# First stage of a hybrid attention step: eight cached sequences compressed one by one in 64 units

## The chip, the cores and the metric

The kernel runs on one core of a Trainium2 chip. The metric is device time of one execution in microseconds (us), as the median of several runs; lower is better. The engines are named as in the profile: PE (TensorE, the matrix products) with PEld (its weight loads), DVE (VectorE), ACT (ScalarE), POOL (GpSimd) and SP (SyncE, which here only issues DMAs). Each engine takes its instructions from a queue of its own, in the order in which the program put them there.

## What is computed

One decode step of a one-layer model: a prompt of 512 rows and eight sample sequences of 8 rows, each sample with 2048 cached tokens in 16 pages of 128 tokens. What matters here is the compression of the cached keys and values of the sparse attention branch, and the start of the layer:

```python
def compress_blocks(x, pos, w1, w2):          # x: 2048 cached tokens of one sequence, 2 groups of 64
    xc = x.reshape(b, n_chunk, 16, NSA_GROUPS, HEAD_DIM)
    lead  = einsum('bncgd,cdh->bngh', xc + pos[0], w1[0])
    trail = einsum('bncgd,cdh->bngh', xc + pos[1], w1[1])
    return einsum('bngh,hd->bngd', silu(lead[:, :-1] + trail[:, 1:]), w2)
...
mod = silu(c) @ w_ada + b_ada                 # conditioning: shift, scale, gate
h = rms_norm(x, norm1_g) * (1.0 + sc1) + sh1  # prompt and sample rows
z = h @ w_in
```

Keys and values (kv = 0, 1) of eight sequences go through `compress_blocks`. Everything after `z` (three attention branches, the output projection, the MLP) is untouched by the change.

## The kernel before, in words

The first stage (`first_stage`, line 512) interleaves two jobs. One is the compression of the eight cached sequences; the other is the work that the projection `z` needs: the norm of x, its transposition, and the first eight blocks of the conditioning `mod` (called ada). The compression is cut into **units**, listed in `self.units` (line 548). A unit is a set of sequences `bs`, a quarter j of the 16 token positions, and kv. The first 16 units handle one sequence each (sequences 0 and 1, eight units per sequence), the other 24 handle two at a time (2 and 3, 4 and 5, 6 and 7): 40 units.

What one unit does:

- `cmp_order` (line 447, DVE): a copy `ro<-cpg` of 128x1024 elements for each sequence, which brings the page tile `cpg` into the order that the transposes want; once for two units (k and v).
- `rows_turn` (line 456): four transposes on PE for each sequence, into a PSUM tile `ct`; then, for each of two halves a, ACT rounds the half to `xh` (128x256) and DVE takes the rest `xl` = ct - xh (128x256). `xh` and `xl` lie in a ring of two units.
- `cmp_hidden` (line 473): twelve products on PE (four weights times the three terms high*high, low*high, high*low), accumulated in the PSUM tile `hid`. A product has 256 columns for one sequence, 512 for two.

The main loop (line 623) runs over u. In round u the program issues `rows_turn(u + 1)`, then `cmp_hidden(u)`, then the jobs in `todo[u]`. PE's order is therefore ct(u+1), hid(u), ct(u+2), hid(u+1) and so on, with the extra products of `todo` between them. `cmp_order(u + 2)` comes before `rows_turn(u + 1)`, except where the next unit begins with a new set of sequences ((u + 2) % 8 == 0, line 636): there it comes after `rows_turn(u + 1)`. With `behind()` (line 535) an instruction is kept behind the last split (`xh`, `xl`) that was issued so far on ACT and on DVE; before the change that holds for `cmp_order` in the units up to 15 and at every change of sequences.

`todo` (lines 570 to 621) holds by unit: the norm of the five tiles of x (`norm`: a square with sum on ACT, 128x1024; some ten small steps and a 128x1024 scaling on DVE), their transposes (`turned`: eight products `nt`, two copies), the ada blocks (`ada_first`, `ada_end`, lines 316 and 303; 1 MB of w_ada each, asked for on POOL's queue), `modulate` (line 752, DVE), and for each two sequences the silu (`cmp_act`: two ACT passes and one DVE pass over 128x512, for k and for v), the second product (`cmp_out`, `co`), the key norm and its transpose (`cmp_keys`, `kct`). `pages(b)` asks on SP's queue for the 16 pages of sequence b, into one of four `cpg` tiles. `asked(f)` (line 581) puts a one-element POOL copy that reads `xl` ahead of an issue on POOL's queue, so that the issue waits for that unit.

The end of the stage is the **seam** (line 2095), called at u == 38, with two units left. It frees the stage's tiles, asks for the first columns of w_in (`winr`), and splits h, eight row blocks `h2[k]`, each one ACT pass (128x576) and two DVE passes (128x512 and 128x64, line 777), and `winh`, `winl` in two halves (one ACT pass and one DVE pass of 128x1056 each). Pins fix the order on ACT and DVE: `h2[0..2]` behind the splits of unit 38, then, behind those of unit 39, half 0 of w_in, `h2[3..4]`, half 1, `h2[5..7]`. The first tile of `z` (24 products, three for each k) follows hid(39) on PE.

Of the kernel before, what the change touches and what calls it, by code (L numbers as in the profile page):

```python
# [18 lines left out]
NB = 8  # L19
# [26 lines left out]
class Step:  # L46
# [465 lines left out]
    def first_stage(self, pl, pe, hf, seam):  # L512


        nc = self.nc
        self.chain = ""
        self.sideb = self.mmb
        self.w1raw, self.cpg, self.ros, self.hid, self.adas = [], {}, {}, {}, {}
        xs = []

        def load_x():
            k = len(xs)
            xs.append(pe.tile([P, D], F32, tag="x", bufs=3, name=f"x{k}"))
            self.dma("gpsimd", xs[k][:TILES[k][1]], self.x_rows(k))

        def norm(k):
            with self.tc.issue_after(self.last_high):
                self.norm_scaled(xs[k], 0, k, xs[k], pl.tile([P, D], BF16, tag="csx", name=f"sq{k}"))

        def turned(k):  # L530
            t0, m = TILES[k]
            for h in range(2):
                self.copy(hf[:, 4 * h:4 * h + 4, t0:t0 + m], self.norm_turned(xs[k], 0, k, h))

        def behind():
            both = ExitStack()
            for i in (self.last_high, self.splits[-1]):
                both.enter_context(self.tc.issue_after(i))
            return both

        def pinned(f):
            def g():
                with behind():
                    f()
            return g


        self.units = [(b // 2, bs, j, kv) for b, bs in ((0, (0,)), (1, (1,)), (2, (2, 3)), (4, (4, 5)), (6, (6, 7)))
                      for j in range(4) for kv in range(2)]
        self.page_rows()  # L550
        for b in range(4):
            self.cmp_tile(pe, b)
        self.cmp_raw(pe, 0)

        warm = self.small.tile([P, 1], F32, tag="warm", bufs=1, name="warm")
        nc.vector.memset(warm, 0.0)
        self.act(warm, warm, AF.Tanh)
        self.cmp_pages("sync", 0, slice(0, 8))
        self.cmp_pages("scalar", 0, slice(8, 16))
        self.cmp_raw(pe, 1)  # L560
        self.cmp_pages("sync", 1)
        self.cmp_weights(pl)
        self.ada_start()
        self.constants()
        self.late_constants()
        self.cmp_pages("sync", 2)
        self.cmp_pages("sync", 3)

        ada, ends = [4, 0, 5, 1, 6, 2, 7, 3], {}
        todo = {u: [] for u in range(40)}  # L570
        todo[9] += [pinned(self.ada_silu)]
        todo[18] += [pinned(self.cmp_second_half)]
        todo[10] += [self.constants_turned, self.ada_turned, lambda: ends.update(b=self.cmp_bias(pe))]
        todo[12] += [lambda: self.cmp_bias_end(ends["b"])]

        for k, u in enumerate((19, 21, 23, 25, 27)):
            todo[u - 2] += [lambda k=k: norm(k)]
            todo[u] += [lambda k=k: turned(k)]
        pages = lambda b: lambda: (self.cmp_tile(pe, b), self.cmp_pages("sync", b))
        wada = lambda k: lambda: self.ada_first_load(pe, ada[k])  # L580
        def asked(f):
            def g():

                x = self.ring[0][1]
                c = nc.gpsimd.tensor_copy(warm, x[:, 0, 0:1].bitcast(F32))
                with self.tc.issue_after(c.ins):
                    f()
            return g

        todo[8] += [pages(4)]  # L590
        todo[9] += [asked(self.cmp_second)]
        todo[14] += [pages(5)]
        todo[15] += [asked(load_x)]
        todo[16] += [load_x, load_x]
        todo[17] += [asked(wada(0))]
        todo[19] += [load_x]
        todo[21] += [load_x]
        todo[23] += [asked(wada(1))]
        todo[24] += [self.late_loads]
        todo[20] += [pages(6)]  # L600
        todo[22] += [pages(7)]
        for k, u in enumerate((22, 25, 27, 29, 31, 32, 34, 35)):
            todo[u] += [lambda k=k: ends.update({k: self.ada_first(pe, ada[k])})]
            todo[u + 1] += [lambda k=k: ends[k]()]
            if k > 1:
                todo[(23, 26, 28, 30, 32, 33)[k - 2]] += [wada(k)]
            if k % 2:
                todo[max(u + 2, 28)] += [lambda k=k: self.modulate(0, hf, range(k - 1, k + 1))]
        self.lfg = {}
        for y, u in enumerate((25, 28)):  # L610
            todo[u] += [pinned(lambda y=y: self.stage_logf(pe, y))]
            todo[u + 2] += [lambda y=y: self.store_logf(y)]
        for i in range(3):
            for kv in range(2):
                todo[8 * i + 14 + kv] += [lambda i=i, kv=kv: self.cmp_act(pl, i, kv)]
        for i in range(3):
            for kv in range(2):
                todo[8 * i + 18 + kv] += [lambda i=i, kv=kv: self.cmp_out(pl, i, kv)]
            todo[8 * i + 21] += [lambda i=i: self.cmp_keys(i)]
        self.cmp_order(pl, 0)  # L620
        self.cmp_taps(0)
        self.rows_turn(0)
        for u in range(40):
            if u % 2 == 0 and u + 2 < 40 and (u + 2) % 8:
                with behind() if u + 2 < 16 else nullcontext():
                    self.cmp_order(pl, u + 2)
            if u + 1 < 8:
                with behind():
                    self.cmp_taps(u + 1)
            if u + 1 < 40:  # L630
                self.rows_turn(u + 1)
            if u == 37:
                self.behind38 = self.splits[-1], self.last_high
            if u == 38:
                seam()
            if (u + 2) % 8 == 0 and u + 2 < 40:

                with behind():
                    self.cmp_order(pl, u + 2)
            self.cmp_hidden(u)  # L640
            for f in todo[u]:
                f()
        self.r1 = self.keep.tile([P, 5 * D], F32, tag="r1", bufs=1, name="r1w")
        with behind():
            for kv in range(2):
                self.cmp_act(pl, 3, kv)
        self.sideb = self.stackb = self.trb
# [1425 lines left out]
    def run(self):  # L2073
# [10 lines left out]
        hf = self.adw[:, 0:NK * NT].rearrange("p (k t) -> p k t", k=NK)  # L2084
# [7 lines left out]
        pl, pe = self.pool("pl", lctx), self.pool("pe", actx)  # L2092
        h2 = []

        def seam():
# [15 lines left out]

            self.wraw = {}
            self.win_load(self.pw, 0)
            rows(self.behind38, range(3))
            for i in range(2):
                self.win_split(self.pw, 0, i, last)
                rows(last, ((3, 4), (5, 6, 7))[i])

        self.first_stage(pl, pe, hf, seam)
        lctx.close()  # L2120
# [133 lines left out]
```

## Time and profile before

| | |
|---|---|
| median of 3 runs | 1231.15 us (1231.12 to 1231.8) |
| the profiled execution, its own time | 1231.5 us |
| its span in the profile | 1229.7 us |
| granted TensorE clock, mean | 0.994 |
| PE busy | 1186.9 us (97%) |
| PEld busy | 1022.7 us (83%) |
| DVE busy | 684.9 us (56%) |
| ACT busy | 513.6 us (42%) |

Rows of the timeline read: start (us from the span's start), length in us, engine, line, operation, output<-input, partitions x elements and count; in brackets how long the engine had been idle before it, and what it had waited for. A row with xN merges N instructions; lengths of PE rows contain the time that a result takes to come out, so starts are compared, not lengths. In rows of the waits stand: who waited for whom, total us, times, longest us.

### The profile page before, as it was taken

Reading aid. Unit: us, or ns where it says so; the run is one execution under the profiler, and the core shown is the slowest. Engines: PE = TensorE matmul, PEld = TensorE weight load, DVE = VectorE, ACT = ScalarE, POOL = GpSimd, SP = SyncE. Lnnn points to the kernel's source line nnn. Section 1 sums busy time; section 2 is a strip of 40 time slices with the busy share of each in tenths; the row PEclk is TensorE's granted clock in tenths of the full one; section 3 lists DMA queues with packets and bytes.
Section 4 is the critical chain, followed back from the end, with each engine's and each line's share of the span. In section 5 each row is a group of like instructions: output and inputs, shape, how many; then the busy total and the mean of one; then the engine's idle time right before and its main releaser. Section 6 shows DMA issues by size and latency. Waiting matters only on the chain.

```text
span 1229.7 us, 24815 instructions
## 1 busy us (share of the span) xinstructions
PE 1186.9 (97%) x9475; PEld 1022.7 (83%) x9475; DVE 684.9 (56%) x1875; ACT 513.6 (42%) x1152; POOL 131.2 (11%) x144
## 2 busy tenths in 40 slices
PE   3899999999999989999999999999999999999998
PEld 3888789999666556666799999998989989899896
DVE  3688785676788845555543445654343433434546
ACT  2455453454777744454432333365423213232230
POOL 1012100001211120000200000001102011020110
PEclk9999999999999899999999999999999999999999
DMA  9589547794866449789763234115314223142202
GB/s 208 160 246 272 161 145 235 245 319 151 287 208 200 132 138 308 255 264 295 172 165 94 78 93 128 29 52 155 103 43 130 69 70 103 53 119 70 69 18 77
DMA packets 170201, 188.11 MB, mean 153 GB/s; under 512 B 16185, under 2 KB 149762, under 8 KB 167906
## 3 DMA queue, kind: packets, MB, share of 16 engines
q1 hardware_dynamic: 157890, 167.13, 44.6%
q0 software_dynamic: 6880, 16.25, 4.4%
q10 hardware_dynamic: 5312, 3.15, 1.2%
q8 instruction: 75, 1.23, 0.4%
q14 instruction: 44, 0.36, 0.1%
HBM read 176.48 MB, written 30.90 MB: 169 GB/s over the span
## 4 chain that ended last, share of the span: by engine, by line
PE 85%; DVE 5%; DMA 4%; SPq 3%; ACT 2%; issue 1%; DVEq 0%; ACTq 0%
PE up L77 17%; PE dn L77 17%; PE mg L77 8%; PE z L77 7%; PE hid L77 5%; PE wo L77 4%; PE br L77 4%; PE ss L77 4%; SPq L155 3%; PE k L83 2%; PE ct L83 2%; PE so L77 2%; DMA cpg<-in_cache_nsa_kv 2%; PE ada L77 1%; PE sp L83 1%
## 5 line engine op out<-in xcount | busy, mean ns | idle before, releaser
L77 PE MATMUL z<-winh,h 128*128 128x264 f32 (+1 forms) x576 | 111.0, 286 | 0.3
L2024 POOL TENSOR_TENSOR u<-u 128x576 f32<-128x576 f32 x32 | 53.4, 1669 | 409.3 <-ACT u L112 318.2
L77 PEld LDWEIGHTS z<-winh,h 128*128 128x128 f32 x576 | 91.7, 190 | 2.1 <-DVE h L777 0.9
L77 PE MATMUL z<-winl,h 128*128 128x264 f32 (+1 forms) x320 | 88.2, 284 | 0.2 <-DVE winl L131 0.2
L100 DVE TENSOR_TENSOR acc<-acc,dn 128x512 f32<-128x512 f32 x60 | 39.8, 685 | 73.0 <-PE dn L77 73.0
L77 PE MATMUL mg<-hH,wmh 128*128 128x288 f32 x256 | 75.9, 298 | 2.0 <-ACT wmh L112 2.0
L77 PE MATMUL mg<-hH,wml 128*128 128x288 f32 x256 | 75.9, 298 | 0.9 <-DVE wml L131 0.9
L112 ACT ACTIVATE xh<-ct 128x256 fp32r<-128x256 f32 x128 | 48.0, 385 | 59.2 <-PE ct L83 35.8
L77 PE MATMUL mg<-hL,wmh 128*128 128x288 f32 x256 | 72.6, 294 | 0.0
L131 DVE TENSOR_TENSOR xl<-ct,xh 128x256 fp32r<-128x256 f32 x128 | 51.6, 420 | 19.4 <-ACT xh L112 17.7
L777 DVE TENSOR_TENSOR u<-u,u 128x512 fp32r<-128x512 f32 x64 | 27.4, 469 | 60.7 <-ACT u L112 60.7
L77 PEld LDWEIGHTS z<-winl,h 128*128 128x128 f32 x320 | 60.6, 190 | 0.4 <-DVE winl L131 0.4
L83 PE MATMUL ct<-identF,ro 128*128 128x128 f32 x256 | 36.3, 281 | 22.7 <-DVE ro L115 22.1
L83 PEld LDWEIGHTS ct<-identF,ro 128*128 128x128 f32 x256 | 29.6, 146 | 26.6 <-DVE ro L115 18.7
L77 PEld LDWEIGHTS mg<-hH,wmh 128*128 128x128 f32 x256 | 48.6, 190 | 2.4 <-ACT wmh L112 2.2
L77 PEld LDWEIGHTS mg<-hH,wml 128*128 128x128 f32 x256 | 48.5, 189 | 1.1 <-DVE wml L131 1.1
L131 DVE TENSOR_TENSOR wml<-wmr,wmh 128x1024 fp32r<-128x1024 f32 x14 | 17.1, 1224 | 56.0 <-ACT wmh L112 55.9
L112 ACT ACTIVATE u<-up 128x256 f32<-128x256 f32 (+1 forms) x96 | 27.8, 325 | 48.7 <-PE up L77 48.7
L77 PEld LDWEIGHTS mg<-hL,wmh 128*128 128x128 f32 x256 | 47.2, 188 | 0.1
L77 PE MATMUL hid<-xh,w1hlk 128*128 128x512 f32 (+1 forms) x160 | 45.0, 369 | 0.1
L77 PE MATMUL hid<-xh,w1hlv 128*128 128x512 f32 (+1 forms) x160 | 43.9, 360 | 0.5 <-ACT xh L112 0.5
L1700 DVE CUSTOM_DVE_ANT_0 sS<-ss,scr 128x512 f32<-128x512 f32 x32 | 22.1, 691 | 30.2 <-PE ss L77 30.2
(951 smaller groups left out, 3584.1 us busy)
## 6 DMA issues: line engine op xcount, KB each, us to landing
adw<-in_w_ada SPq DMA_DIRECT2D x16, 1024.0 KB
foxD<-in_cache_fox_kv SPq DMA_DIRECT2D x128, 128.0 KB
wur<-in_w_up SPq DMA_DIRECT2D x32, 512.0 KB
wdr<-in_w_down SPq DMA_DIRECT2D x32, 512.0 KB
cpg<-in_cache_nsa_kv SPq DMA_DIRECT2D x120, 128.0 KB
fr<-foxD SPq DMA_DIRECT2D x28, 512.0 KB
sr<-in_cache_nsa_kv SPq DMA_DIRECT2D x112, 128.0 KB
wada<-in_w_ada POOLq DMA_DIRECT2D x8, 1024.0 KB, 6.3
```

Of the source, the lines that this page charges most:

```text
L77: ins = self.nc.tensor.matmul(out, a, b, start=start, stop=stop, skip_group_check=True)
L83: ins = self.nc.tensor.transpose(out, in_, self.identF[:n, :n])
L100: self.nc.vector.tensor_tensor(out, a, b, op=op)
L112: return self.nc.scalar.activation(out, in_, f, **kw)
L131: self.splits.append((eng or self.nc.vector).tensor_tensor(l, x, h.bitcast(F32), op=OP.subtract).ins)
L155: self.issued[eng] = getattr(self.nc, eng).dma_start(out, in_).ins
L777: self.packed = (eng or self.nc.vector).tensor_tensor(h2[:, o:o + n], x[:, i:i + n], h2[:, i:i + n].bitcast(F32), op=OP.subtract).ins
L1700: self.nc.vector.tensor_tensor_reduce(self.S[u], pb, self.ramp[:, 512 * i:512 * i + 512], 1.0, LOW, OP.add, OP.max, self.stat[b][0][:, i / ...
L2024: nc.gpsimd.tensor_tensor(u[j], u[j], u[j], op=OP.mult)
```

## The change

All eight sequences get units of their own: 64 units, sequence b in units 8b to 8b + 7, so all products `hid` have 256 columns. The jobs in `todo` are placed anew over 64 units: norms at 19, 23, 27, 31, 35 and their transposes three units later, ada blocks at 29 to 56, silu and second product every 16 units. Pages of sequences 5 to 7 are asked for at units 14, 22, 30. Counted in units, the rows of x and the blocks of w_ada are asked for further ahead of their use. `cmp_order` of all units is now kept behind the last splits. The seam is called at u == 62, again with two units left; `h2[0]` is pinned behind the splits of unit 61, `h2[1]` behind those of unit 62, and half 0 of w_in, `h2[2..4]`, half 1 and `h2[5..7]` behind those of unit 63.

```diff
-        self.units = [(b // 2, bs, j, kv) for b, bs in ((0, (0,)), (1, (1,)), (2, (2, 3)), (4, (4, 5)), (6, (6, 7)))
-                      for j in range(4) for kv in range(2)]
+        self.units = [(b // 2, (b,), j, kv) for b in range(NB) for j in range(4) for kv in range(2)]
+        N = len(self.units)
...
-        for k, u in enumerate((19, 21, 23, 25, 27)):
-            todo[u - 2] += [lambda k=k: norm(k)]
+        for k, u in enumerate((22, 26, 30, 34, 38)):
+            todo[u - 3] += [lambda k=k: norm(k)]
             todo[u] += [lambda k=k: turned(k)]
...
-        todo[8] += [pages(4)]
+        for b in range(4, NB):
+            todo[8 * (b - 4) + (8 if b == 4 else 6)] += [pages(b)]
         todo[9] += [asked(self.cmp_second)]
-        todo[14] += [pages(5)]
         todo[15] += [asked(load_x)]
-        todo[16] += [load_x, load_x]
-        todo[17] += [asked(wada(0))]
-        todo[19] += [load_x]
-        todo[21] += [load_x]
-        todo[23] += [asked(wada(1))]
-        todo[24] += [self.late_loads]
-        todo[20] += [pages(6)]
-        todo[22] += [pages(7)]
-        for k, u in enumerate((22, 25, 27, 29, 31, 32, 34, 35)):
+        todo[16] += [load_x]
+        todo[18] += [load_x]
+        todo[20] += [asked(wada(0))]
+        todo[23] += [load_x]
+        todo[25] += [asked(wada(1))]
+        todo[27] += [load_x]
+        todo[28] += [self.late_loads]
+        for k, u in enumerate((29, 34, 39, 43, 47, 50, 53, 56)):
             todo[u] += [lambda k=k: ends.update({k: self.ada_first(pe, ada[k])})]
             todo[u + 1] += [lambda k=k: ends[k]()]
-            if k > 1:
-                todo[(23, 26, 28, 30, 32, 33)[k - 2]] += [wada(k)]
+            if k < 6:
+                todo[u + 1] += [wada(k + 2)]
             if k % 2:
-                todo[max(u + 2, 28)] += [lambda k=k: self.modulate(0, hf, range(k - 1, k + 1))]
+                todo[max(u + 2, 40)] += [lambda k=k: self.modulate(0, hf, range(k - 1, k + 1))]
...
-        for u in range(40):
-            if u % 2 == 0 and u + 2 < 40 and (u + 2) % 8:
-                with behind() if u + 2 < 16 else nullcontext():
+        for u in range(N):
+            if u % 2 == 0 and u + 2 < N and (u + 2) % 8:
+                with behind():
                     self.cmp_order(pl, u + 2)
...
-            if u == 37:
-                self.behind38 = self.splits[-1], self.last_high
-            if u == 38:
+            if N - 4 <= u < N - 2:
+                self.ahead.append((self.splits[-1], self.last_high))
+            if u == N - 2:
                 seam()
...
-            rows(self.behind38, range(3))
+            rows(self.ahead[0], (0,))
+            rows(self.ahead[1], (1,))
             for i in range(2):
                 self.win_split(self.pw, 0, i, last)
-                rows(last, ((3, 4), (5, 6, 7))[i])
+                rows(last, ((2, 3, 4), (5, 6, 7))[i])
```

## The prediction on record

> **What bounds the kernel now.** I read the page's busy shares first, then busy time by stretches, then the waits and PE's timeline for the first 190 us. The sequence of PE's products behind the first stage is the same in both programs, so the change is decided before the first product of `z`.
>
> ```profile
> span 1229.7 us, 24815 instructions
> ...
> PE 1186.9 (97%) x9475; PEld 1022.7 (83%) x9475; DVE 684.9 (56%) x1875; ACT 513.6 (42%) x1152; POOL 131.2 (11%) x144
> ...
> 62.50:100.00 37.50, 37.44 (x230) 31.19 (x229) 31.59 (x118) 22.25 (x53) 6.97 (x12) 1.00 0.89 247
> ...
> PE ct L83 <- DVE ro L115: 22.1, 4, 18.7
> ```
>
> PE is busy for 97% of the span, and in a stretch inside the stage for 37.44 of 37.5 us. Of PE's waits in the first 190 us only one group is large, transposes that wait for DVE's copy `ro`: 22.1 us, of which 18.7 are the start, before any page has been copied. That leaves 3.4 us. No row of x and no block of w_ada stands among what PE waited for, so asking for them sooner has nothing to remove. The stage is a chain of PE products with few holes; what counts is PE's work, and whether ACT and DVE have each unit ready in time.
>
> **The change part by part.**
>
> *Pace of PE.* In the next rows x4 is a unit of one sequence, x8 one of two.
>
> ```profile
> 39.94 0.60 PE L83 MATMUL ct<-identF,ro 128*128 128x128 f32 x4
> ...
> 40.30 0.48 PE L77 MATMUL hid<-xh,w1hlk 128*128 128x256 f32 x2
> ...
> 41.83 0.60 PE L83 MATMUL ct<-identF,ro 128*128 128x128 f32 x4
> ...
> 65.56 1.06 PE L83 MATMUL ct<-identF,ro 128*128 128x128 f32 x8
> ...
> 66.38 0.71 PE L77 MATMUL hid<-xh,w1hlv 128*128 128x512 f32 x2
> ...
> 69.24 1.04 PE L83 MATMUL ct<-identF,ro 128*128 128x128 f32 x8
> ...
> 160.52 1.04 PE L83 MATMUL ct<-identF,ro 128*128 128x128 f32 x8
> ...
> 164.21 0.38 PE L83 MATMUL kct<-identF,knn 128*128 128x128 f32 x2
> ```
>
> Narrow unit: 41.83 - 39.94 = 1.89 us, of it 0.36 for the transposes and 1.53 for the twelve 256-column products. Wide unit: 3.68 us from 65.56 to 69.24, 2.86 of it for the twelve 512-column products. Of the 21 such starts of wide units with nothing else between them (first and last above, 3.68 and 3.69) the mean is 3.73. The other products between the units (`nt`, `co`, `kct`, `ada`, `adat`) are the same in number. From the first hid of unit 16 to the first of `z`, before: 22 x 3.73 + 2 x 2.86 = 87.8 us. After: 48 x 1.53 + 46 x 0.36 = 90.0. The cost is **+2.2 us**.
>
> A rule speaks against narrow products here. The Trainium skill, "TensorE: Matmul & The Clock Gate", section "Back-to-back issue gap", has sustained spacings of about 81 ns at 128 columns and 131 ns at 512. An estimate from these two figures puts 256 columns near 98 ns, so two narrow products would take 1.49 times one wide one and the change would cost 24 x 2.86 x 0.49 = 34 us. The trace disagrees: 2 x 1.53 / 2.86 = 1.07. I go by the trace.
>
> *The start of the first pair.* Before, ct(16) needs copies for both sequences:
>
> ```profile
> 54.61 0.60 PE L83 MATMUL ct<-identF,ro 128*128 128x128 f32 x4
> ...
> 57.80 0.63 PE L83 MATMUL ct<-identF,ro 128*128 128x128 f32 x4 [1.14 <-DVE ro L115]
> ...
> 59.23 0.63 PE L83 MATMUL ct<-identF,ro 128*128 128x128 f32 x4 [0.79 <-DVE ro L115]
> ...
> 61.64 1.06 PE L83 MATMUL ct<-identF,ro 128*128 128x128 f32 x8 [0.35 <-DVE xl L131]
> ...
> 62.46 0.71 PE L77 MATMUL hid<-xh,w1hlk 128*128 128x512 f32 x2
> ...
> 56.60 0.42 DVE L131 TENSOR_TENSOR xl<-ct,xh 128x256 fp32r<-128x256 f32 x1 [0.45 <-ACT xh L112]
> ...
> 56.97 0.69 DVE L115 COPY ro<-cpg 128x1024 f32<-128x1024 f32 x1
> ...
> 58.39 1.29 DVE L115 COPY ro<-cpg 128x1024 f32<-128x1024 f32 x2 [0.73 <-DMA cpg<-in_cache_nsa_kv]
> ```
>
> The first half of ct(16) starts at 57.80, the second waits for the second copy (page data of sequence 3: DVE idle 0.73) until 59.23, and ct(17) waits 0.35 for `xl`; the first product of unit 16 starts at 62.46. After: ct(16) at 57.80 as before, 0.36 + 1.53 (hid 15) + 0.36 (ct 17), hid(16) at 60.05. **-2.4 us**. The 1.14 us at 57.80 stay: that copy is behind the last split of unit 15 in both programs.
>
> *The same wait at five more places.* The three rows of DVE say what that wait is: the copy for a new sequence stands behind the last `xl` of the unit before (56.60, then 56.97), and ct(16) follows the copy's end. From ct(15) to ct(16) are 57.80 - 54.61 = 3.19 us instead of 1.89: **1.30 us** lost. The chain that ends there, for a narrow unit:
>
> ```profile
> 40.58 0.39 ACT L112 ACTIVATE xh<-ct 128x256 fp32r<-128x256 f32 x1 [0.59 <-PE ct L83]
> ...
> 41.45 0.39 ACT L112 ACTIVATE xh<-ct 128x256 fp32r<-128x256 f32 x1 [0.49 <-DVE xl L131]
> ...
> 41.00 0.42 DVE L131 TENSOR_TENSOR xl<-ct,xh 128x256 fp32r<-128x256 f32 x1
> ...
> 41.87 0.42 DVE L131 TENSOR_TENSOR xl<-ct,xh 128x256 fp32r<-128x256 f32 x1 [0.45 <-ACT xh L112]
> ```
>
> Within a unit ACT and DVE take turns, each waiting for the other: `xh` 40.58, `xl` 41.00, `xh` 41.45 (0.49 idle for `xl`), `xl` 41.87 to 42.29. That is 2.35 us after its transposes began at 39.94. Add 0.69 for a copy and the hand-over, and the next sequence's transposes cannot start before 3.1 to 3.2 us, while PE needs them after 1.89. A wide unit gave PE 3.7 us. In DVE's queue of the changed program the first copy for sequences 3, 4, 5, 6 and 7 stands right behind the last `xl` of units 23, 31, 39, 47 and 55. What hides it is only what PE has between: `nt` of one x tile ahead of ct(24), ct(32) and ct(40), and `adat` ahead of ct(32) and ct(56); nothing ahead of ct(48).
>
> ```profile
> 96.27 1.04 PE L83 MATMUL nt<-identF,x 128*128 128x128 f32 x8
> ...
> 97.14 0.38 PE L83 MATMUL adat<-identF,adap 128*128 128x128 f32 x2
> ...
> 97.36 1.04 PE L83 MATMUL ct<-identF,ro 128*128 128x128 f32 x8
> ```
>
> `nt` takes 97.14 - 96.27 = 0.87, `adat` 0.22. Left over: 0.43, 0.21, 0.43, 1.30, 1.08, together **+3.45 us**. Bounds: half of it, 1.7, if PE is itself held up shortly before and the copies catch up; 5 x 1.30 = 6.5 if nothing covers (`nt` needs the scaled x, which stands in the same DVE queue).
>
> *Bursts with a shorter look-ahead.* The last `xl` of a narrow unit is ready at 2.35 us, and the first product that reads it (the sixth of twelve) comes at 2 x 1.89 - 1.53 + 0.6 = 2.85 us after that unit's transposes began: 0.5 us to spare. Into this go, over 48 units, five norms, three key norms, four `modulate` and the silus:
>
> ```profile
> 33.08 0.50 PE L77 MATMUL hid<-xh,w1hlv 128*128 128x256 f32 x2 [0.46 <-ACT xh L112]
> ...
> 94.84 1.05 ACT L112 ACTIVATE sq<-x 128x1024 bf16<-128x1024 f32 x1
> ...
> 102.92 0.74 DVE L104 TENSOR_SCALAR x<-x,nrs 128x1024 f32<-128x1024 f32 x1
> ```
>
> One square holds ACT for 1.05 us, one scaling DVE for 0.74. Neither fits into 0.5 us. Nothing in the old trace shows them in narrow units; the nearest row is in units 1 to 7, which also carried a split of the weights each: there PE lost 0.46 us (at 33.08) in seven units. 48 units at that rate: **+3.2 us**; that is my value. Below it 0: DVE has free time over the stage, and 20 us of extra products lie on PE in the same units. Above, twice as much, 6.4.
>
> *The end of the stage.* Both programs call the seam two units before the end, but a unit is half as long now.
>
> ```profile
> 164.43 1.03 PE L83 MATMUL ct<-identF,ro 128*128 128x128 f32 x8
> ...
> 170.88 0.40 PE L77 MATMUL z<-winh,h 128*128 128x264 f32 x2
> ...
> 174.95 0.41 PE L77 MATMUL z<-winh,h 128*128 128x264 f32 x2
> ...
> 177.86 1.00 PE L77 MATMUL co<-w2rawk,r1w 128*128 128x64 f32 x8
> ...
> 167.47 1.08 ACT L112 ACTIVATE winh<-winr 128x1056 fp32r<-128x1056 f32 x1
> ...
> 168.44 1.25 ACT L112 ACTIVATE h<-adw 128x576 fp32r<-128x576 f32 x2
> ...
> 171.23 1.25 DVE L131 TENSOR_TENSOR winl<-winr,winh 128x1056 fp32r<-128x1056 f32 x1
> ...
> 172.40 2.29 DVE L777 TENSOR_TENSOR h<-adw,h 128x512 fp32r<-128x512 f32 x6
> ```
>
> Before, the last transposes start at 164.43; the last `xh` is done when `winh` starts at 167.47, 3.41 us ahead of `z` at 170.88. From there ACT and DVE have two halves of w_in (1.1 to 1.25 us each) and five row blocks (0.6 each on ACT, 2.29 / 3 = 0.76 on DVE) to split, down to 174.69 on DVE. The first tile of `z` runs behind them: 174.95 - 170.88 = 4.07 us instead of the next tile's 177.86 - 174.95 = 2.91. After, ct(63) starts 0.36 + 2 x 1.53 = 3.42 us ahead of `z`, and its last `xh` ends 1.90 later (39.94 to 41.45 + 0.39), so only 1.52 us are left instead of 3.41: 1.9 us later. Six row blocks instead of five are behind it: 0.76 more. And h2[1] now stands on ACT ahead of that `xh`: 0.6. Sum **+3.3 us**; from 1.9 (start alone) to 4.0 (h2[1] costs its DVE passes too).
>
> *Moved issues.* A 1 MB block of w_ada takes this long on POOL's queue from issue to landing:
>
> ```profile
> wada<-in_w_ada POOLq DMA_DIRECT2D x8, 1024.0 KB, 6.3
> ```
>
> Each block is asked for one unit after the sum that frees its place and is used at least five units later, 9.5 us of PE time against 6.3: hidden, with some 3 us to spare; if the cover goes, PE waits for the difference. The rows of x are half as large. On POOL the later issues (conditioning, gathers) stand in the same order behind them. On SP the pages of sequences 6 and 7 are asked for when the copies of 2 and 3 free their tiles, 26 narrow units (49 us) ahead of use; before, those of 7 came 10 wide units (37 us) ahead, and PE waited for neither. The stores of log forget values stand ahead of `winr` as before. I take all of these at nothing.
>
> *Sum.* -2.4 + 2.2 + 3.45 + 3.2 + 3.3 = **+9.75 us**. The profiled execution took 1231.5 us with a span of 1229.7 us; the median is 0.35 lower, 1231.15. 1231.5 + 9.75 - 0.35 = **1240.9 us**.
>
> **The rivals.**
>
> - *Only the end costs.* The five boundary waits and the bursts vanish behind PE's other products; 1231.15 - 0.2 + 3.3 = 1234.3 us. For it: DVE and ACT are not full. Against: ct(48) and ct(56) have next to nothing ahead of them.
> - *Look-ahead too short throughout.* Each of 14 bursts costs 0.5 us and no boundary is covered: -0.2 + 6.5 + 7 + 3.3 = 16.6, 1247.8 us. Against: units 1 to 7 lost only 0.46.
> - *Bare rate (the faster side).* The tile of `z` above ran 24 products of 264 columns in 2.91 us, 0.121 each. If narrow units ran so, a pair would take 2 x (12 x 0.121 + 0.36) = 3.62 instead of 3.73: 24 x 0.11 = 2.6 us gained, with the 2.4 at the start 5 us: 1226.1 us. It decides if boundaries, bursts and end together stay under 2.5 us. Against: narrow units with nothing in the way took 1.89, and the end alone is put at 3.3.
> - *Only PE's work changes.* -2.4 + 2.2, nothing else: 1231 us. That is also the case in which asking sooner and spreading out does what it says and no wait is added.
> - *Weight loads no longer hidden.*
>
> ```profile
> L77 PEld LDWEIGHTS hid<-xh,w1hlk 128*128 128x128 f32 x160 | 28.0, 197 | 3.7 <-ACT xh L112 0.4
> ```
>
> A load takes 197 ns; twelve of them 2.4 us against 1.53 measured for a narrow unit's products. If PE had to wait for them: 0.8 x 48 = 40 us more, about 1271. Against: the narrow units of the trace hide them. The rule of the Trainium skill quoted above, from "TensorE: Matmul & The Clock Gate", points this way.
>
> **How the numbers follow.** Forecast 0.66, only the end 0.12, look-ahead too short 0.09, bare rate 0.08, PE's work alone 0.04, weight loads 0.01. A measurement of this kernel tells about 0.2% (2.5 us) from no change. Faster by more than that: 0.08. Within it: 0.04. Slower: 0.88. Low end of the range: -0.2 + 1.7 + 0 + 1.9 = 3.4, with the rival at 1234.3 taken in: 1234 us. High end: -0.2 + 6.5 + 6.4 + 4.0 = 16.7: 1248 us. Outside lie the faster side and little else, about 0.15. The likeliest case's own range is 1236 to 1246.
>
> **What the next profile would show.** All 768 `hid` products with 256 columns, 1.5 us for twelve. Transposes that wait for `ro` at eight starts of PE instead of four, most for about 1 us, the longest at ct(48) and ct(56). PE idle on `xh` or `xl` in units 17 to 39 by a few tenths each. The first tile of `z` over 6 us long, with starts that follow DVE's h splits. No wait of PE for a DMA. I am wrong if the first tile of `z` takes under 4.5 us, or if ct(48) starts within 2.2 us of ct(47); and, the other way, if PE waits for x, w_ada or pages.

## The result, and the profile after

The changed kernel takes 1243.08 us (median of 4 runs, 1241.84 to 1244.66), the kernel before, run beside it, 1231.13 us (4 runs, 1228.1 to 1231.8). The ratio is 1.0103, 95% interval 1.0082 to 1.0123: **slower by about 1%**, 12 us; forecast were 9.75 us.

The page of the changed kernel opens with its span and the busy shares:

```profile
span 1241.1 us, 25367 instructions
...
PE 1190.7 (96%) x9763; PEld 1038.5 (84%) x9763; DVE 687.3 (55%) x1875; ACT 515.1 (42%) x1152; POOL 130.8 (11%) x144
```

PE has 288 more instructions and is busy for 3.8 us more; the span grew by 11.4. Two thirds of the loss is therefore PE standing still. Where it stands still, PE's timeline shows (start, length, ..., in brackets the idle time and what ended it):

```profile
54.93 0.60 PE L83 MATMUL ct<-identF,ro 128*128 128x128 f32 x4
58.13 0.63 PE L83 MATMUL ct<-identF,ro 128*128 128x128 f32 x4 [1.15 <-DVE ro L115]
60.01 0.60 PE L83 MATMUL ct<-identF,ro 128*128 128x128 f32 x4
60.36 0.48 PE L77 MATMUL hid<-xh,w1hlk 128*128 128x256 f32 x2
...
66.37 1.10 PE L77 MATMUL co<-w2rawk,cst 128*128 128x64 f32 x8 [0.52 <-DVE w2rawk L104]
...
86.10 1.09 PE L83 MATMUL nt<-identF,x 128*128 128x128 f32 x8 [0.61 <-DVE x L104]
...
105.71 1.09 PE L83 MATMUL nt<-identF,x 128*128 128x128 f32 x8 [0.76 <-DVE x L104]
...
116.53 0.44 PE L83 MATMUL kct<-identF,knn 128*128 128x128 f32 x2 [1.01 <-DVE ntt L100]
...
120.36 0.63 PE L83 MATMUL ct<-identF,ro 128*128 128x128 f32 x4 [0.86 <-DVE ro L115]
...
136.30 0.60 PE L83 MATMUL ct<-identF,ro 128*128 128x128 f32 x4
139.50 0.63 PE L83 MATMUL ct<-identF,ro 128*128 128x128 f32 x4 [1.15 <-DVE ro L115]
...
176.83 0.60 PE L83 MATMUL ct<-identF,ro 128*128 128x128 f32 x4
...
180.88 0.40 PE L77 MATMUL z<-winh,h 128*128 128x264 f32 x2
...
187.73 0.41 PE L77 MATMUL z<-winh,h 128*128 128x264 f32 x2
```

The reader is to see four things. The start of the third sequence is short now: ct(16) at 58.13, the first product of unit 16 at 60.36. At 139.50 stands ct(48), 3.20 us after ct(47) instead of 1.89, waiting for `ro`. Between lie waits of 0.5 to 1 us for `w2rawk`, for the scaled `x` and for the key norm (`ntt`). And the first tile of `z` runs from 180.88 to 187.73, 6.85 us instead of 4.07.

For the third point, the same four products in the kernel before, none of which waits:

```profile
73.01 1.10 PE L77 MATMUL co<-w2rawk,cst 128*128 128x64 f32 x8
...
86.69 1.04 PE L83 MATMUL nt<-identF,x 128*128 128x128 f32 x8
...
105.12 1.04 PE L83 MATMUL nt<-identF,x 128*128 128x128 f32 x8
...
126.90 0.44 PE L83 MATMUL kct<-identF,knn 128*128 128x128 f32 x2
```

For the fourth, DVE after the change. The row blocks of h stand between and behind the two halves of w_in, and the second tile starts at 187.73, 0.27 us after the last of them is done (185.16 + 2.30 = 187.46), as it did before (174.69 and 174.95):

```profile
180.61 1.26 DVE L131 TENSOR_TENSOR winl<-winr,winh 128x1056 fp32r<-128x1056 f32 x1 [0.73 <-ACT winh L112]
181.79 2.29 DVE L776 TENSOR_TENSOR h<-adw,h 128x512 fp32r<-128x512 f32 x6
184.00 1.26 DVE L131 TENSOR_TENSOR winl<-winr,winh 128x1056 fp32r<-128x1056 f32 x1
185.16 2.30 DVE L776 TENSOR_TENSOR h<-adw,h 128x512 fp32r<-128x512 f32 x6
```

ct(16) itself comes 0.32 us later in this execution, before anything differs, so I count from ct(16). In these terms (differences of starts in the timelines; "tile" is the time from the first product of one tile of `z` to the first of the next):

| | ct(16) to z | first tile | second tile | sum |
|---|---|---|---|---|
| before | 113.08 | 4.07 | 3.72 | 120.87 |
| after | 122.75 | 6.85 | 4.42 | 134.03 |

The stage lost 13.2 us, while the whole span lost 11.4: in these two executions the rest of the program took 1.8 us less after the change. Most of that lies 420 us later, where the branch mixing `mg` waits for a split weight, first before, then after the change:

```profile
PE mg L77 <- ACT wmh L112: 2.0, 1, 2.0
```

```profile
PE mg L77 <- ACT wmh L112: 0.7, 1, 0.7
```

Ahead of it the shift of PE's products had grown to 14.0 us (a wait for a window load `wr`: 2.75 instead of 2.19 us), behind it it is 11.4 and stays there to the end. It is tempting to say that a PE that arrives later waits less, but the other traces don't bear this out. What is late is a load of w_in, for which ACT is idle ahead of the split (6.32 us before, 5.08 after). The wait of `mg` behind it is 0.9 us in the experiment "the earlier copy in the kernel before", where `z` starts at 171.18, and 2.3 us in "four sequences narrow", where it starts at 174.50. From the third tile of `z` to the end, the thirteen profiles of this case take between 1047.7 and 1051.1 us, with the same PE products there: 1051.1 before, 1048.9 after, 1048.2 in that kernel with the earlier copy. So the 1.8 us are within what this part differs by from profile to profile; that the change gives them back is not shown. Below I therefore judge the first stage by the trace and the whole by medians.

### The profile page after: what moved, and what is told of

Its sections match the earlier page's. It is cut to its first block, busy times and chain, and to the rows that moved or that the text cites. A ratio compares the mean times of both kernels' runs of the same rounds, so it can differ in the third digit from the quotient of the medians.

```text
span 1241.1 us, 25367 instructions
## 1 busy us (share of the span) xinstructions
PE 1190.7 (96%) x9763; PEld 1038.5 (84%) x9763; DVE 687.3 (55%) x1875; ACT 515.1 (42%) x1152; POOL 130.8 (11%) x144
## 4 chain that ended last, share of the span: by engine, by line
PE 84%; DVE 5%; DMA 5%; ACT 3%; SPq 2%; issue 1%; DVEq 0%; ACTq 0%
PE up L77 16%; PE dn L77 16%; PE mg L77 8%; PE z L77 8%; PE wo L77 4%; PE br L77 4%; PE ss L77 4%; PE hid L77 3%; DMA cpg<-in_cache_nsa_kv 3%; PE k L83 2%; PE so L77 2%; SPq L155 2%; PE ada L77 2%; PE ct L83 1%; PE sp L83 1%
## 5 line engine op out<-in xcount | busy, mean ns | idle before, releaser
L83 PE MATMUL ct<-identF,ro 128*128 128x128 f32 x256 | 40.0, 281 | 24.8 <-DVE ro L115 23.8
L77 PE MATMUL hid<-xh,w1hlk 128*128 128x256 f32 x256 | 51.8, 300 | 0.1
L77 PE MATMUL hid<-xh,w1hlv 128*128 128x256 f32 x256 | 50.3, 292 | 0.5 <-ACT xh L112 0.4
L77 PEld LDWEIGHTS hid<-xh,w1hlk 128*128 128x128 f32 x256 | 40.4, 195 | 0.4 <-ACT xh L112 0.4
```

Of the source, the lines that this page charges most:

```text
L77: ins = self.nc.tensor.matmul(out, a, b, start=start, stop=stop, skip_group_check=True)
L83: ins = self.nc.tensor.transpose(out, in_, self.identF[:n, :n])
```

## The experiments

My theory was the prediction's: narrow products cost PE almost nothing, and the loss is waits, at the boundaries between sequences, behind bursts on ACT and DVE, and at the seam. The rival: narrow units are slower by themselves (PE, ACT and DVE can't supply them), and a wait taken away shows up again elsewhere.

**Copies ahead of the splits.** In the changed kernel the first copy of sequences 3 to 7 is put ahead of the splits of the unit before:

```diff
-            if u % 2 == 0 and u + 2 < N and (u + 2) % 8:
+            if u % 2 == 0 and u + 2 < N and ((u + 2) % 8 or u + 2 > 16):
...
-            if (u + 2) % 8 == 0 and u + 2 < N:
+            if (u + 2) % 8 == 0 and u + 2 <= 16:
```

> The changed kernel with one edit: the first copy ro for sequences 3 to 7 is issued one unit earlier, as for all other units (before the transposes of the unit ahead, not behind their splits). Wait theory (the loss is made of waits at the changes of sequence, of bursts on ACT and DVE, and of the late seam): the five waits at ct(24), ct(32), ct(40), ct(48), ct(56), 4.15 us in the changed kernel's trace, go; the first product of z moves from 180.9 to about 176.8 us, the median from 1243 to about 1239. Pace theory (narrow units are slow in themselves, the waits only show where PE is ahead of its supply): the wait turns up elsewhere in the same units, z starts later than 179.5, median within 1.5 us of 1243.

Measured: 1240.04 us (4 runs, 1238.73 to 1242.55; ratio to the kernel before 1.0085, 1.0053 to 1.0118). ct(16) to z fell from 122.75 to 120.81. PE's timeline:

```profile
116.81 0.44 PE L83 MATMUL kct<-identF,knn 128*128 128x128 f32 x2 [1.66 <-DVE ntt L100]
...
135.62 0.60 PE L83 MATMUL ct<-identF,ro 128*128 128x128 f32 x4
137.51 0.60 PE L83 MATMUL ct<-identF,ro 128*128 128x128 f32 x4
...
157.27 0.41 PE L83 MATMUL kct<-identF,knn 128*128 128x128 f32 x2 [0.61 <-DVE knn L100]
```

ct(47) and ct(48) are 1.89 us apart: the largest boundary wait has gone to nothing, and those ahead of ct(40) and ct(56) with it; only ct(24), which also waits for `nt`, kept its 0.4. Together 3.5 us went. But the key norm's transpose now waits 1.66 instead of 1.01, and another 0.61, and two units lost 0.2 to 0.3: 1.8 us came back. Both theories have a part: the waits are what the prediction said, and removing them moves a copy ahead of other work that was itself only just in time.

**The last pair in wide units.** Sequences 0 to 5 one by one, 6 and 7 together, 56 units, the seam's pins as before the change. The last four ada blocks move with it, one of them to the place ahead of ct(48), and the copies `ro` within the wide units are free of the pin to the last splits again:

```diff
-        self.units = [(b // 2, (b,), j, kv) for b in range(NB) for j in range(4) for kv in range(2)]
+        self.units = [(b // 2, bs, j, kv) for b, bs in [(b, (b,)) for b in range(6)] + [(6, (6, 7))] for j in range(4) for kv in range(2)]
...
-        for k, u in enumerate((29, 34, 39, 43, 47, 50, 53, 56)):
+        for k, u in enumerate((29, 34, 39, 43, 46, 48, 50, 51)):
...
-                with behind():
+                with behind() if u + 2 < 48 else nullcontext():
...
-            rows(self.ahead[0], (0,))
-            rows(self.ahead[1], (1,))
+            rows(self.ahead[1], range(3))
...
-                rows(last, ((2, 3, 4), (5, 6, 7))[i])
+                rows(last, ((3, 4), (5, 6, 7))[i])
```

> The changed kernel with sequences 6 and 7 compressed as a pair again (48 narrow units and 8 wide ones, 56 in all), the seam two wide units before the end and pinned as before the change. Wait theory: the first tile of z takes about 4.1 us instead of 6.85, the hold-ups by h2[0] and h2[1] in the last units (0.47 and 0.63) and the wait at ct(56) (1.1) go, some 0.5 us come back from the pace: median near 1237.5. Pace theory: the eight pairs give back a third of the loss up to z, 3 to 4 us, and the first tile of z stays at 6.5 us or more: median near 1239.5.

Measured: 1235.71 us (9 runs, 1234.09 to 1237.54; ratio 1.0043, 1.0024 to 1.0062). PE at the seam:

```profile
170.35 1.04 PE L83 MATMUL ct<-identF,ro 128*128 128x128 f32 x8
...
176.81 0.40 PE L77 MATMUL z<-winh,h 128*128 128x264 f32 x2
...
180.88 0.40 PE L77 MATMUL z<-winh,h 128*128 128x264 f32 x2
```

From 176.81 to 180.88 the first tile of `z` takes 4.07 us, as before the change: the whole 2.8 us at that place go with a wide last unit and the old pins. The run doesn't tell these two apart, so how much of the 2.8 us is the shorter time behind the last transposes alone stays open. ct(16) to z fell to 119.17, the sum to the third tile to 126.96. One pair out of three made wide gave back 7.1 of the stage's 13.2 us, because the boundaries ahead of ct(48) and ct(56) and the seam are all in it; ahead of ct(48) there is now an ada block as well. The median is 1.8 us lower than the wait theory had it.

**No norm.** This kernel leaves out the norm of x in the first stage:

```diff
         def norm(k):
             with self.tc.issue_after(self.last_high):
-                self.norm_scaled(xs[k], 0, k, xs[k], pl.tile([P, D], BF16, tag="csx", name=f"sq{k}"))
+                pass
```

> The changed kernel without the norm of x in the first stage (x is transposed and used as it was loaded: no square, no small steps, no scaling). It leaves out five bursts on ACT (1.2 us each) and DVE (some 2 us each). Wait theory: PE's waits for the scaled x (0.61 and 0.76) go and the wait at ct(40) falls from 1.0 to 0.4 or less: z starts 2 to 3 us sooner than 180.9. Rival (bursts hide in DVE's free time, the waits come from the change of sequence alone): under 1 us sooner.

Measured: 1242.2 us in one run; ct(16) to z 120.14, 2.6 less, as the wait theory had it. On PE:

```profile
114.06 0.44 PE L83 MATMUL kct<-identF,knn 128*128 128x128 f32 x2
...
117.54 0.63 PE L83 MATMUL ct<-identF,ro 128*128 128x128 f32 x4 [0.53 <-DVE ro L115]
```

The waits of `nt` for `x` are gone, and so is the 1.01 us of `kct`, whose small steps had stood behind the norm's on DVE (0.45 of it appears at a `hid` instead). ct(40) waits 0.53 instead of 0.86. So the norms alone are worth 2.6 us of the stage in narrow units. The span of this one execution is only 0.7 us shorter (1240.4), as the part behind the stage took longer.

**Loads asked for later.** In the changed kernel, four of the five loads of rows of x and the first two blocks of w_ada are asked for one to three units later:

```diff
-        todo[16] += [load_x]
         todo[18] += [load_x]
-        todo[20] += [asked(wada(0))]
-        todo[23] += [load_x]
-        todo[25] += [asked(wada(1))]
-        todo[27] += [load_x]
+        todo[19] += [load_x]
+        todo[23] += [asked(wada(0))]
+        todo[25] += [load_x]
+        todo[28] += [asked(wada(1))]
+        todo[29] += [load_x]
```

> The changed kernel with the rows of x and the first two blocks of w_ada asked for one to three units later. Wait theory and pace theory: nothing, z starts within 0.5 us of 180.9 and PE waits for no DMA. If asking sooner is worth something, PE, ACT or DVE waits for x or w_ada now and z starts over 1 us later.

Measured: 1242.1 us in one run, ct(16) to z 122.65, against 122.75: nothing, and no wait of PE for one of these loads. The earlier asking that the change brought bought nothing here.

**All of h behind the last split.** In the changed kernel, no row block of h ahead of unit 63's `xh`:

```diff
-            rows(self.ahead[0], (0,))
-            rows(self.ahead[1], (1,))
...
-                rows(last, ((2, 3, 4), (5, 6, 7))[i])
+                rows(last, ((0, 1, 2, 3, 4), (5, 6, 7))[i])
```

> The changed kernel with all eight row blocks of h behind the splits of unit 63 (none ahead of the last xh). If h2[0] and h2[1] ahead of those splits cost PE 0.47 at ct(61) and 0.63 between ct(63) and z: z starts 1.1 us sooner counted from ct(16). The first tile of z grows by two row blocks on DVE, 2 x 0.76 = 1.5 us, to 8.4 us. Together +0.4: 1243.5 us. Rival (the first tile of z isn't bound by DVE's h splits but by w_in): its length stays at 6.9, 1242.

Measured: 1243.27 us (5 runs, 1243.01 to 1245.19; ratio 1.0117, 1.01 to 1.0133). One row of PE's timeline near unit 60, then one of DVE's:

```profile
171.76 0.39 PE L77 MATMUL hid<-xl,w1hlv 128*128 128x256 f32 x1 [0.23 <-DVE xl L131]
```

```profile
180.77 5.25 DVE L776 TENSOR_TENSOR h<-adw,h 128x512 fp32r<-128x512 f32 x14
```

Half of my reading fell: the 0.47 us between ct(60) and ct(61) are still there, so they are not h2[0]'s; the row at 171.76 stands right behind the last `modulate` on DVE and is a burst. h2[1] cost 0.3 at `z`, not 0.6. The other half held: seven row blocks on DVE (14 passes, 5.25 us) now stand between the two halves of w_in, the first tile of `z` takes 9.42 us, and from ct(16) to the third tile it is 135.88 instead of 134.03, 1.8 us more where 1.5 less 1.1 was expected. The time is nevertheless that of the changed kernel within what can be told: from the third tile to the end this execution took 1047.7 us, the changed kernel's 1048.9 (waits for `wr`: 1.4 us instead of 2.8).

**Four sequences narrow.** Sequences 0 to 3 one by one, two pairs, 48 units, jobs of `todo` moved accordingly; the aim was to keep the gain at ct(16) and shed the rest:

```diff
-        self.units = [(b // 2, (b,), j, kv) for b in range(NB) for j in range(4) for kv in range(2)]
+        self.units = [(b // 2, bs, j, kv) for b, bs in [(b, (b,)) for b in range(4)] + [(4, (4, 5)), (6, (6, 7))] for j in range(4) for kv in range(2)]
```

> Sequences 0 to 3 one by one, (4,5) and (6,7) in pairs: 48 units, seam pins of the kernel before, copies of ro as before. Wait theory: the start of sequence 2 gains 2.4 us as in the change, one pair in narrow units costs 0.7 (8 x (2 x 1.89 - 3.69)), the wait at ct(24) behind nt 0.45, three norms between narrow units some 0.8, the wait for two copies at ct(32) is covered by ada and nt (0 to 0.5), the first tile of z stays at 4.1 us: together 0 to -0.5, about 1230.8 us beside 1231.1 for the kernel before. Rival (narrow units themselves are slower than their bare spacing, whatever waits): 16 narrow units instead of 48 leave a third of the change's loss outside its end, about +2.5: 1233.5.

Measured: 1235.12 us (6 runs, 1232.91 to 1238.27; ratio 1.0048, 1.003 to 1.0066); ct(16) to z 116.44, 3.4 more than before. A miss. PE:

```profile
86.03 1.09 PE L83 MATMUL nt<-identF,x 128*128 128x128 f32 x8 [0.62 <-DVE x L104]
...
97.35 1.23 PE L83 MATMUL ct<-identF,ro 128*128 128x128 f32 x8 [0.81 <-DVE ro L115]
...
100.73 1.10 PE L83 MATMUL ct<-identF,ro 128*128 128x128 f32 x8 [0.51 <-DVE adas L308]
```

The start that a pair needs (two copies, then splits of double size) did not go away, it moved from ct(16) to ct(32) and cost 0.81 and 0.51 there in spite of `nt` and `ada` ahead of it. And in the 16 narrow units spacings over 1.89 us plus the products between were lost at `co` (0.8), at `kct` (0.6), at ct(24) (0.4) and at `nt` (0.8). The undisturbed spacing is again 1.86 to 1.90 us, so it isn't the narrow product that is slow: the rival's size came nearer, its mechanism didn't.

**The same with earlier copies** at units 8 and 24:

```diff
-            if u % 2 == 0 and u + 2 < N and (u + 2) % 8:
+            if u % 2 == 0 and u + 2 < N and ((u + 2) % 8 or u + 2 in (8, 24)):
...
-            if (u + 2) % 8 == 0 and u + 2 < N:
+            if (u + 2) % 8 == 0 and u + 2 < N and u + 2 not in (8, 24):
```

> The kernel of the four narrow sequences, with the first copy of sequences 1 and 3 put ahead of the splits of the unit before (units 8 and 24; unit 16 as it was). Wait theory: ct(8) starts 1.3 to 1.5 us sooner (it waited 1.5), ct(24) 0.3 to 0.5, nothing given back: 1.7 us less than the same kernel without it, about 1229.1, the first version below the kernel before. Rival (DVE's copy only moves the wait to the xl behind it): the next units lose what the boundary gains, 1230.8.

Measured: 1233.88 us (11 runs, 1231.03 to 1236.09; ratio 1.0037, 1.0025 to 1.0048). ct(8) came 1.64 us sooner behind ct(7) (1.89 instead of 3.53) and all of it reached `z` (172.63 instead of 174.50); ct(24) gained nothing, as it waits for the scaled `x` as well. The median fell by 1.2 us where 1.7 was expected, and stays above the kernel before.

**The earlier copy in the kernel before.** Only the condition at unit 8:

```diff
-            if u % 2 == 0 and u + 2 < 40 and (u + 2) % 8:
+            if u % 2 == 0 and u + 2 < 40 and ((u + 2) % 8 or u + 2 == 8):
...
-            if (u + 2) % 8 == 0 and u + 2 < 40:
+            if (u + 2) % 8 == 0 and u + 2 < 40 and u + 2 != 8:
```

> The kernel before with only the first copy of sequence 1 put ahead of the splits of unit 7. ct(8) starts 1.3 to 1.5 us sooner. If what sets the start of the first pair is DVE's order alone, the gain stays: 1229.7 us. If it is the landing of the pages of sequence 3 (DVE idle 0.73 for cpg in the kernel before), the gain is given back at the second half of ct(16), DVE is idle there for about 2 us, and the time stays at 1231.1.

Measured: 1231.09 us beside 1229.91 (12 and 22 runs; ratio 1.0016, 1.0004 to 1.0028). First DVE, then PE:

```profile
55.38 0.69 DVE L115 COPY ro<-cpg 128x1024 f32<-128x1024 f32 x1
57.71 1.30 DVE L115 COPY ro<-cpg 128x1024 f32<-128x1024 f32 x2 [1.63 <-DMA cpg<-in_cache_nsa_kv]
```

```profile
56.22 0.63 PE L83 MATMUL ct<-identF,ro 128*128 128x128 f32 x4 [1.14 <-DVE ro L115]
58.55 0.97 PE L83 MATMUL ct<-identF,ro 128*128 128x128 f32 x4 [1.70 <-DVE ro L115]
```

ct(16) starts 1.6 us sooner, its second half only 0.7, and `z` not at all (171.18): DVE waits 1.63 us for the pages of sequence 3. The second expectation held in the trace (the median is even a little higher): in the kernel before, the start of the first pair is bound by a transfer. On which part of it, two more rows of the kernel before say something, SP's queue and the windows view (length, busy time of PE, PEld, DVE, ACT, POOL, clock, share of the DMA engines, GB/s):

```profile
2.95 59.39 SPq L155 DMA_DIRECT2D cpg<-in_cache_nsa_kv  x64
```

```profile
55.00:60.00 5.00, 3.07 (x25) 2.69 (x24) 3.25 (x7) 2.58 (x6) 0.00 (x0) 1.00 0.50 159
```

SP issues 64 pages in 59.39 us, 0.93 each on average, one after the other. The 41st to the 56th are those of sequence 3, the last eight of sequence 4; the last page of sequence 3 is issued at 55.35 us and the second copy starts at 58.39. From 15 to 25 us the DMA engines were full (shares of 1.17 and 1.14), but from 30 to 60 us SP issues a page every 0.83 us and the engines' share is 0.53. This points to the issuing as what is late; the next runs test it.

**Pages on a second queue.** The kernel before, with half of sequence 3's pages on POOL's queue behind unit 2; in the first version with the earlier copy at unit 8, in the second with those at unit 16 as well, in the third with none:

```diff
-        self.cmp_pages("sync", 3)
+        self.cmp_pages("sync", 3, slice(0, 8))
...
+        todo[2] += [asked(lambda: self.cmp_pages("gpsimd", 3, slice(8, 16)))]
```

> The kernel before with the first copy of sequence 1 ahead of the splits of unit 7 (as in the run before it), and with the second half of sequence 3's pages asked for on POOL's queue, behind unit 2, instead of at the end of SP's, which issued pages without a break until 62.3 us (one in 0.93 us). If the start of the first pair was bound by those issues: DVE doesn't wait for cpg, the second half of ct(16) follows one copy (0.69) behind the first, ct(8) keeps its 1.6 us; z starts 2.3 us sooner than in the kernel before (168.6 in the profile), 1228.8 us beside 1231.1 (or beside 1229.9, the median of that kernel on the other chip: 2.3 less). Rival (the transfers themselves are bound, two queues share the same engines, and the pages of sequences 0 to 2 come later by what those of 3 gain): nothing gained, the time of the kernel before.

Measured: **1228.43 us** beside 1231.09 (12 and 22 runs; ratio 0.9981, 0.997 to 0.9993), with `z` at 168.54 where 168.6 was expected. DVE, then PE:

```profile
55.34 2.08 DVE L115 COPY ro<-cpg 128x1024 f32<-128x1024 f32 x3
```

```profile
56.18 0.63 PE L83 MATMUL ct<-identF,ro 128*128 128x128 f32 x4 [1.15 <-DVE ro L115]
56.97 0.63 PE L83 MATMUL ct<-identF,ro 128*128 128x128 f32 x4 [0.16 <-DVE ro L115]
59.39 1.06 PE L83 MATMUL ct<-identF,ro 128*128 128x128 f32 x8 [0.35 <-DVE xl L131]
```

Three copies run without a break, no wait for `cpg`: the pages were bound by when they were asked for. This version is below both kernels. How far below is less sure: the kernel before itself had 1229.91 in the experiment ahead of this one.

> The same, and both copies for the first pair (unit 16) also ahead of the splits of unit 15. Wait theory: the 1.14 us at ct(16) and the 0.7 behind it go, and 0.3 to 0.8 comes back because 1.3 us of copies stand ahead of the xl of unit 15, which has 0.5 to spare: z starts 3.3 us sooner than in the kernel before (167.6), 3.3 us less in all. Rival (DVE's order decides nothing any more once the pages are there, because xl of unit 15 and 16 are then late by the same): as the kernel without it, 2.3 less.

Measured: 1228.37 us (11 runs; ratio 0.9978, 0.9969 to 0.9988), but `z` at 171.01, 2.5 later than without the further copies. DVE, then PE:

```profile
52.48 0.69 DVE L115 COPY ro<-cpg 128x1024 f32<-128x1024 f32 x1 [1.63 <-DMA cpg<-in_cache_nsa_kv]
```

```profile
53.56 0.38 PE L77 MATMUL hid<-xl,w1hlv 128*128 128x256 f32 x1 [1.53 <-DVE xl L131]
```

The copy for sequence 3 was asked for so soon that its pages were not there again; DVE stood still with the `xl` of unit 13 queued behind the copy, and PE lost 1.53 us there and more at ct(15). The edit does not keep these copies behind any split (`behind()` holds for units below 16), so they ran ahead of unit 13's and not only of unit 15's. Neither expectation gave this. The median is nevertheless as low as that of the version without; the profile shows one execution, and it was the slowest of the eleven (1230.68 us).

> The kernel before with only the second half of sequence 3's pages on POOL's queue, all copies of ro as in the kernel before. If the earlier version gained at the start of the stage: ct(8) still waits 1.5 us, only the second half of ct(16) comes 0.6 us sooner, z starts 0.6 sooner, and the time is 0.6 us (0.05%) below the kernel before, not to be told from it. Rival (the shorter queue on SP gains in the later part of the program, whatever the first stage does, which would explain that the version whose z is no sooner was as fast): 2.7 us less, 0.2%, with z only 0.6 sooner.

Measured: 1229.73 us beside 1230.04 (12 and 17 runs; ratio 0.9999, 0.9986 to 1.0011): the second queue alone changes nothing that can be told, as the first expectation had it. `z` starts at 169.99, 0.9 us sooner where 0.6 was expected, against 2.3 with the earlier copy. By the traces the gain of the first version therefore belongs to the earlier copy together with the sooner pages; by the medians alone it isn't shown, as the two intervals overlap. Why the second version, whose `z` comes no sooner in its profile, is as fast stays open; several profiles of it would be needed.

No run takes out the pins that keep every copy `ro` behind the last splits, which the change extended to all units. The changed kernel's trace speaks against a cost: all six waits of transposes for `ro` stand at the first unit of a sequence, and these copies were kept behind the splits before the change as well (the first one of all needs no pin).

## Why the prediction was right, and where it was off

Sign and size held, and so did the main reading: narrow products cost PE little, and the loss is waits at boundaries, behind bursts and at the seam. How the bursts would make PE wait was read wrongly. The sum was 9.75 us; the median grew by 12 us and the span of the profiled execution by 11.4. By its own steps:

| step | predicted | measured |
|---|---|---|
| start of the first pair | -2.4 | -2.4 |
| pace of narrow units | +2.2 | about +2.2 (spacing 1.85 to 1.93) |
| five boundaries | +3.45 | +4.16 |
| bursts | +3.2 | +5.2 |
| end, seam | +3.3 | +4.1 |
| sum, first stage | +9.75 | 13.3 from the terms, 13.2 in the trace |
| rest of the program | none | -1.8 between these two executions, not shown to be the change's |

- *Start.* From ct(16) to the first product of unit 16 were 4.66 us before (57.80 to 62.46) and are 2.23 now (58.13 to 60.36). Right.
- *Pace.* Undisturbed narrow units follow each other in 1.85 to 1.93 us in the changed kernel. The two extreme rivals fell with it: the bare rate (0.121 us for a product would make 1.81) and the weight loads. The latter was the one that leaned on the Trainium skill, "TensorE: Matmul & The Clock Gate", section "Back-to-back issue gap". The trace does not agree with the estimate of 1.49 that was made from its figures: the twelve 256-column products take 1.53 us here as before, 0.128 each, against 2.86 for twelve of 512, so two narrow ones cost 1.07 times a wide one.
- *Boundaries.* What the spacing exceeds 1.89 plus the products between: 0.45, 0.27, 1.02, 1.32, 1.10 at ct(24), 32, 40, 48, 56, where 0.43, 0.21, 0.43, 1.30, 1.08 were forecast. Only ct(40) was off: its `nt` is that of the 64-row tile, shorter than the 0.87 us that I credited (0.64 before), and steps of the norm stood in the same queue of DVE. The profile counts six waits for `ro`, not eight: the one at ct(56) is put down to `adas`, though it is gone in the run with the earlier copies, and none is listed at ct(32):

```profile
PE ct L83 <- DVE ro L115: 23.8, 6, 18.9
```

- *Bursts* is the step that was mis-sized most, inside its bounds of 0 to 6.4. I priced them as a rate of lost time per unit taken from units 1 to 7, and had PE idle for `xh` or `xl` by a few tenths in many units. Between ct(16) and `z` the profile lists one such wait, 0.2 us. The runs showed that PE waits for the jobs' own products instead (excess of the spacing at each): `co` 0.8, `kct` 0.6 and 1.2, `nt` 0.8, a unit with `nt`, `ada` and `co` 1.35, the `xl` behind a `modulate` 0.5. What the first ones have in common is a distance between a job and its use that is counted in units, while a unit lasts half as long. `kct` stands two to three units behind `co` in both kernels, `nt` three behind `norm` instead of two (5.7 us instead of 7.4), and `co` in the same round as the scaling of its weights. That reading fits these rows; tested alone were only the norms (2.6 us).
- *End.* 0.63 ahead of `z`, 2.78 in its first tile, 0.70 in its second. The main term, less time behind the last `xh`, agrees with the wide last pair (first tile back at 4.07), which had the old pins as well. The term for h2[1] ahead of `xh` was too high (0.3 for 0.6), and I counted the first tile only.
- *Moved issues.* Nothing, as forecast: from ct(16) to `z` no wait of PE for a DMA, and later loads changed 0.1 us.
- *Sum.* "The sequence of PE's products behind the first stage is the same" was true, but the terms for the stage were 3.5 us too low. That the sum is nearer to what the whole program lost (11.4 to 12 us) is luck: the rest of the program happened to take 1.8 us less in the changed kernel's profile, which no step foresaw. In the later experiments the kernel before had medians of 1229.7 to 1231.1 us, so the loss may as well be 13 us.

The two signs named as fatal didn't appear: the first tile of `z` took 6.85 us (not under 4.5), and ct(48) came 3.20 us behind ct(47) (not within 2.2).

## What to carry to other kernels

Halving the work item of a software pipeline halves the time that every distance in its schedule stands for: look-ahead, prologue of the next stage, and chains of small steps that were placed so many items ahead. PE's own cost was the smaller part here (2 us of 13). At the boundaries between sequences the waits could be read off the old trace, by comparing the length of the dependent chain with the new item's length (3.45 us forecast, 4.16 measured); the same was not tried for `co`, `kct` and `nt`, and there the forecast was furthest off. And when a wait goes but nothing is gained, look at what is late next: here a copy moved 1.6 us forward only met a page that had not landed, as SP had asked for it late, and asking on a second queue made the gain real (0.2% by the medians, 2.3 us at `z`).

## What I had not expected of the hardware

A queue can be bound by its issuing while the DMA engines stand half idle: from 30 to 60 us SP issued a 128 KB page every 0.83 us at an engine share of 0.53, and asking for eight pages on POOL's queue removed DVE's wait. And with PE at 97% and the same products, the part of the program behind the first stage took between 1047.7 and 1051.1 us in thirteen profiles, without following how late the stage ended. A gain or a loss of 2 us in the stage can't be read off the total of one execution.
